# A plain first block pair in every feed-forward stage, with the Strassen sums of the activations made behind it

## The chip, the cores and the metric

The kernel runs on one core of a Trainium2 chip. Its engines work side by side and meet through semaphores: TensorE (PE in the profile) multiplies matrices, VectorE (DVE) and ScalarE (ACT) work element by element, GpSimd (POOL) does a little, and SyncE (SP) issues the DMAs from HBM to SBUF, the on-chip memory. Matmuls add up in PSUM. The metric is the device time of one execution in microseconds (us).

## What is computed

Two layers of an encoder, for one sequence of 512 tokens (`SEQ`) with 1024 channels (`D_MODEL`), all in float32. The change touches the feed-forward stages alone; there are four, two in each layer:

```python
FFN_HIDDEN = ((8 * D_MODEL // 3 + 255) // 256) * 256     # 2816

def swiglu(x, w_gate, w_up, w_down):
    return (jax.nn.silu(x @ w_gate) * (x @ w_up)) @ w_down

for l in range(DEPTH):                                   # DEPTH = 2
    h = x + 0.5 * swiglu(rms_norm(x, ffn1_norm[l]), ffn1_w_gate[l], ffn1_w_up[l], ffn1_w_down[l])
    z = rms_norm(h, mix_norm[l]) @ w_in[l]
    ...
    h = h + jnp.concatenate([y_sgu, y_mlstm], axis=-1) @ w_out[l]
    x = h + 0.5 * swiglu(rms_norm(h, ffn2_norm[l]), ffn2_w_gate[l], ffn2_w_up[l], ffn2_w_down[l])
return rms_norm(x, final_norm)
```

`rms_norm` multiplies by the gain g and by 1/sqrt(mean of squares + eps) of the token.

## The kernel before

**Numbers as two halves.** A float32 matrix is split in a rounded part (hi) and a remainder (lo), and a product is three matmuls: hi x hi, hi x lo, lo x hi. For weights the rounding is a cast on ACT (L144, to `whi` or `whix`) and the remainder a subtraction on DVE (L145, to `wlo` or `wlox`). The pairs `whix`/`wlox` and `whi`/`wlo` take turns, block by block; there are 2 buffers of the x kind and 3 of the other, 3 of `rawx` and 3 of `raw` for what the DMAs bring.

**Activations.** They lie transposed, channels on the partitions, in 8 tiles x[d] of 128 channels by 512 tokens. `Wide.split` (L351) takes them in twos, j = 0 to 3. With the gain multiplied in (`fa`, four pieces of 256 columns) it makes the blocks A11, A12, A22 as hi and lo (L367, L368), then four sums S1, S2, S4, S3 in `fb` (L369), and those as hi and lo (L374, L375).

**Pairs.** The hidden channels are worked in 11 pairs q of 256 channels. A pair computes gate and up products as a 2 x 2 block product in the form of Strassen and Winograd: seven block products of 24 matmuls with 256 columns each (`strassen`, L159 to L161), 168 matmuls, in three PSUM banks pa, pe, pb. The seven need sums of the four weight blocks (`combine`, L149; `pair_plan` yields e0 to e6 in the order in which they are used). A plain pair has eight block products, 192 matmuls, and needs none of the sums. The first stage's pair 0 is plain already (L1048 to L1062, finished by `gated_plain`). The others open with `strassen_pair(..., opening)`, which takes three block products together, first for j = 0, 1, 2, then for j = 3.

**Stage.** The pairs come in groups of 4, 4 and 3, each followed by eight down-projections `pd` (L206 to L208), which are added to x (L598). Four tiles on, the squares that the norm needs are summed on DVE (L293, `acc`); `rstd_tok` sums them over the channels on PE (`ss`, L304), takes the inverse root by Newton steps on 128 x 4 numbers (L222 to L224), puts it on a diagonal (`dg`, L312), and `spread` has PE broadcast it (`rb`, L317). In the first stage `rstd` (L328 to L336) does that on 128 x 512 numbers with a reciprocal.

**Order.** A tile framework puts the instructions of each engine in a row when the kernel is built, by its model of when each is ready; the engine then works its row strictly in order. `take()` hands out weight units and keeps a few more in preparation than are used (`AHEAD`).

Of the kernel before, what the change touches and what calls it, by code (L numbers as in the profile page):

```python
# [8 lines left out]
F32 = mybir.dt.float32  # L9
# [25 lines left out]
class Net:  # L35
    AHEAD = {"X": 4, "M": 2, "F": 2}
# [17 lines left out]
    def masks(self):  # L54
# [4 lines left out]
        make_identity(nc, self.ident)  # L59
        self.tri = []  # L60
# [280 lines left out]
A11, A12, A22, S3, S1, S2, S4 = range(7)  # L341


class Wide(Norm):
    def __init__(self, b, g):
        super().__init__(b, g)
        self.d = 0
        self.eng = b.nc.vector
        self.spread = None

    def split(self, x):  # L351
# [25 lines left out]
        self.last = fa  # L377
# [87 lines left out]
def strassen_pair(b, norm, rstd, opening):  # L465
# [29 lines left out]
    if spread is not None:  # L495
        spread()
# [6 lines left out]
    return halved(b, G, True), rstd  # L503


def pair_plan(blocks):
    st = {}

    def e0(b):
        st["b11"] = b.load(blocks[0])  # L510
        return b.halves(st["b11"])

    def e1(b):
        st["b12"] = b.load(blocks[1])
        b.combine(st["b11"], st["b12"], st["b11"])
        return b.halves(st["b11"])

    def e2(b):
# [653 lines left out]
```

## Time and profile before

| | us |
|---|---|
| median of 3 runs | 1793.61 (1792.57 to 1794.6) |
| the profiled execution | 1797.66 |
| its span | 1795.9 |
| PE busy | 1759.7 (98%) |
| DVE busy | 1396.1 (78%) |
| ACT busy | 868.7 (48%) |

Stage 1 begins its pairs at 7.26 us of the span, stage 2 at 544.05 (behind the output projection of the first mixer), stage 3 at 897.30 (behind the down-projections of stage 2), stage 4 at 1427.02. A group of rows below gives the window from there to the first down-projection for each; for stage 1 the window begins behind its plain pair, at 31.55. In windows, a name with (x) is busy time and number of instructions, PEclk the granted clock of TensorE as a share of full speed. In a timeline a row gives start, duration, engine, line, operation, what is written and read, and in brackets how long the engine had stood before and who released it.

### The profile page before, as it was taken

Reading aid. Unit: us, or ns where it says so; the run is one execution under the profiler, and the core shown is the slowest. Engines: PE = TensorE matmul, PEld = TensorE weight load, DVE = VectorE, ACT = ScalarE, POOL = GpSimd, SP = SyncE. Lnnn points to the kernel's source line nnn. Section 1 sums busy time; section 2 is a strip of 40 time slices with the busy share of each in tenths; the row PEclk is TensorE's granted clock in tenths of the full one; section 3 lists DMA queues with packets and bytes.
Section 4 is the critical chain, followed back from the end, with each engine's and each line's share of the span. In section 5 each row is a group of like instructions: output and inputs, shape, how many; then the busy total and the mean of one; then the engine's idle time right before and its main releaser. Section 6 shows DMA issues by size and latency. Waiting matters only on the chain.

```text
span 1795.9 us, 28343 instructions
## 1 busy us (share of the span) xinstructions
PE 1759.7 (98%) x11626; PEld 1610.3 (90%) x11626; DVE 1396.1 (78%) x2113; ACT 868.7 (48%) x1223; POOL 98.6 (5%) x164
## 2 busy tenths in 40 slices
PE   8999999999998999999989999999999999999998
PEld 8889989887888989989889899898888799899898
DVE  8967958667988957958889588595698989597685
ACT  7434424557555524525545244254576545254255
POOL 6100000103010000000010000002030000000000
PEclk9999999999998999999999999999999999999999
DMA  5332322321241333323323223223112224233223
GB/s 188 95 129 87 122 86 80 97 82 47 66 146 59 114 110 95 118 82 93 108 95 118 82 90 124 89 75 106 59 60 83 91 86 129 84 105 118 83 77 109
DMA packets 51394, 173.60 MB, mean 97 GB/s; under 512 B 5824, under 2 KB 7872, under 8 KB 51264
## 3 DMA queue, kind: packets, MB, share of 16 engines
q1 hardware_dynamic: 51264, 171.79, 29.9%
q8 instruction: 91, 1.49, 0.3%
q14 instruction: 39, 0.32, 0.1%
HBM read 169.67 MB, written 2.10 MB: 96 GB/s over the span
## 4 chain that ended last, share of the span: by engine, by line
PE 85%; DVE 9%; ACT 3%; issue 1%; DMA 1%; SPq 0%; POOL 0%; DVEq 0%; ACTq 0%; POOLq 0%
PE pd L206 9%; PE pd L208 9%; PE pd L207 9%; PE pb L159 6%; PE pb L160 6%; PE pb L161 6%; PE pe L160 4%; PE pa L159 4%; PE pa L160 4%; PE pe L159 4%; PE pa L161 4%; PE pe L161 4%; PE pm L206 3%; PE pm L207 3%; PE pm L208 3%
## 5 line engine op out<-in xcount | busy, mean ns | idle before, releaser
L179 ACT CAST whi<-raw 128x1024 fp32r<-128x1024 f32 (+2 forms) x157 | 151.9, 967 | 317.9 <-PE pd L207 157.5
L206 PE MATMUL pd<-hh,whi 128*128 128x512 f32 (+1 forms) x752 | 282.9, 377 | 0.4 <-ACT hh L448 0.4
L207 PE MATMUL pd<-hl,whi 128*128 128x512 f32 (+1 forms) x752 | 282.6, 376 | 0.6 <-DVE hl L449 0.6
L208 PE MATMUL pd<-hh,wlo 128*128 128x512 f32 (+1 forms) x752 | 282.6, 376 | 0.5 <-DVE wlo L180 0.5
L180 DVE TENSOR_TENSOR wlo<-raw,whi 128x1024 fp32r<-128x1024 f32 (+2 forms) x157 | 176.4, 1125 | 30.0 <-ACT whi L179 29.1
L598 DVE SCALAR_TENSOR_TENSOR x<-pd,x 128x512 f32<-128x512 f32 x88 | 60.7, 690 | 152.1 <-PE pd L208 152.0
L206 PEld LDWEIGHTS pd<-hh,whi 128*128 128x128 f32 x752 | 141.4, 188 | 29.5 <-ACT hh L448 4.3
L208 PEld LDWEIGHTS pd<-hh,wlo 128*128 128x128 f32 x752 | 141.6, 188 | 26.0 <-DVE wlo L180 0.8
L207 PEld LDWEIGHTS pd<-hl,whi 128*128 128x128 f32 x752 | 141.6, 188 | 26.0 <-DVE hl L449 0.8
L144 ACT CAST whi<-rawx 128x1024 fp32r<-128x1024 f32 x86 | 88.6, 1048 | 150.1 <-DVE rawx L149 92.0
L159 PE MATMUL pb<-xh,whix 128*128 128x256 f32 x528 | 153.2, 290 | 4.3 <-ACT u L482 3.4
L161 PE MATMUL pb<-xh,wlox 128*128 128x256 f32 x528 | 151.3, 287 | 0.6 <-DVE wlox L145 0.6
L160 PE MATMUL pb<-xl,whix 128*128 128x256 f32 x528 | 151.3, 286 | 0.0
L144 ACT CAST whix<-rawx 128x1024 fp32r<-128x1024 f32 x86 | 89.8, 1049 | 114.8 <-PE pb L160 80.1
L159 PE MATMUL pb<-xh,whi 128*128 128x256 f32 x504 | 142.2, 282 | 0.1
L160 PE MATMUL pb<-xl,whi 128*128 128x256 f32 x504 | 142.1, 282 | 0.0
L161 PE MATMUL pb<-xh,wlo 128*128 128x256 f32 x504 | 141.5, 281 | 0.5 <-DVE wlo L145 0.5
L144 ACT CAST whi<-raw 128x1024 fp32r<-128x1024 f32 x64 | 67.1, 1048 | 103.0 <-issue 40.5
L145 DVE TENSOR_TENSOR wlo<-rawx,whi 128x1024 fp32r<-128x1024 f32 x86 | 105.1, 1222 | 9.2 <-ACT whi L144 8.9
L145 DVE TENSOR_TENSOR wlox<-rawx,whix 128x1024 fp32r<-128x1024 f32 x86 | 105.0, 1221 | 9.1 <-ACT whix L144 9.1
L159 PEld LDWEIGHTS pb<-xh,whix 128*128 128x128 f32 x528 | 103.0, 195 | 5.8 <-ACT u L482 4.2
L159 PE MATMUL pe<-xh,whi 128*128 128x256 f32 x352 | 101.9, 290 | 5.4 <-ACT xh L374 5.4
(331 smaller groups left out, 5065.7 us busy)
## 6 DMA issues: line engine op xcount, KB each, us to landing
rawx<-in_wst SPq DMA_DIRECT2D x86, 512.0 KB, 3.6
raw<-in_wst SPq DMA_DIRECT2D x86, 512.0 KB, 3.6
raw<-in_wd SPq DMA_DIRECT2D x64, 512.0 KB, 3.6
raw<-in_wd SPq DMA_DIRECT2D x37, 384.0 KB, 3.1
raw<-in_win SPq DMA_DIRECT2D x24, 512.0 KB, 3.5
raw<-in_wo SPq DMA_DIRECT2D x16, 512.0 KB, 3.5
raw<-in_wv SPq DMA_DIRECT2D x8, 512.0 KB, 3.5
x<-in_xT SPq DMA_DIRECT2D x8, 256.0 KB, 4.0
```

What stands on the lines that cost most here:

```text
L144: self.copied = nc.scalar.copy(hi, raw)
L145: nc.vector.tensor_tensor(out=lo, in0=raw, in1=hi.bitcast(F32), op=ALU.subtract)
L159: nc.tensor.matmul(o, whi[:, j, i, :], hi, start=f, stop=False, skip_group_check=True)
L160: nc.tensor.matmul(o, whi[:, j, i, :], lo, start=False, stop=False, skip_group_check=True)
L161: nc.tensor.matmul(o, wlo[:, j, i, :], hi, start=False, stop=j == 3, skip_group_check=True)
L179: self.copied = nc.scalar.copy(hi[:, r], raw[:, r])
L180: nc.vector.tensor_tensor(out=lo[:, r], in0=raw[:, r], in1=hi[:, r].bitcast(F32), op=ALU.subtract)
L206: nc.tensor.matmul(ps, whi[:, k0 + k, :], xh, start=k == 0, stop=False)
L207: nc.tensor.matmul(ps, whi[:, k0 + k, :], xl, start=False, stop=False)
L208: nc.tensor.matmul(ps, wlo[:, k0 + k, :], xh, start=False, stop=k == n - 1)
L598: nc.vector.scalar_tensor_tensor(out=xd, in0=pd, scalar=0.5, in1=xd, op0=ALU.mult, op1=ALU.add)
```

## The change

- Pair 0 of every feed-forward stage is plain (`plain_plan`, `plain_step`, `plain_banks`). The blocks come in the x kind, the other, the x kind, the other. The low half of the fourth activation block, `a21`, is made in `split` from the `hy` pool.
- `split` makes no sums. `sums()` is called after the plain pair and makes them in place in `fa`: two subtractions and two scalar_tensor_tensor of 256 columns for each j, then the cast and the remainder as before.
- `rstd_tok` is called behind `sums` in all stages; `between`, with `spread` and `gated_plain`, runs in pair 1 behind its first block product.
- Signs: the weights' sums are additions, and U is made with scalar_tensor_tensor, two per pair. The count of weight steps is the same.
- `AHEAD` for "X" is 5, and `eye()` makes the identity earlier. `rawx` is taken by b11 and b22, `raw` by b12 and b21. `add` is defined and not called.

```diff
-    AHEAD = {"X": 4, "M": 2, "F": 2}
+    AHEAD = {"X": 5, "M": 2, "F": 2}
...
-    def load(self, src):
-        raw = self.rawx()
+    def load(self, src, chain=False):
+        raw = (self.phase.tile([P, 1024], F32, tag="rawx", name="rawx", bufs=3) if chain else
+               self.wp.tile([P, 1024], F32, tag="raw", name="raw"))
...
-    def combine(self, out, a, c):
-        self.nc.vector.tensor_tensor(out=out, in0=a, in1=c, op=ALU.subtract)
...
-A11, A12, A22, S3, S1, S2, S4 = range(7)
+A11, A12, A22, S3, S2, S4, S1 = range(7)
...
-        fb = b.wide("fb").rearrange("p (q t) -> p q t", q=4)
+        if d % 4 == 1:
+            self.a21 = b.pair(F32R, "a21").rearrange("p k (l t) -> p k l t", l=2)
+        a21 = self.a21[:, d // 2 % 2]
         nc.scalar.copy(hi[:, 0:3], fa[:, 1:4])
+        nc.scalar.copy(a21[:, 0], fa[:, 0])
         nc.vector.tensor_tensor(out=lo[:, 0:3], in0=fa[:, 1:4], in1=hi[:, 0:3].bitcast(F32), op=ALU.subtract)
-        sub = lambda o, a, c, op=ALU.subtract: nc.vector.tensor_tensor(out=fb[:, o - S3], in0=a, in1=c, op=op)
-        sub(S1, fa[:, 0], fa[:, 3], ALU.add)
-        sub(S2, fb[:, S1 - S3], fa[:, 1])
-        sub(S4, fa[:, 2], fb[:, S2 - S3])
-        sub(S3, fa[:, 1], fa[:, 0])
-        nc.scalar.copy(hi[:, 3:7], fb)
-        nc.vector.tensor_tensor(out=lo[:, 3:7], in0=fb, in1=hi[:, 3:7].bitcast(F32), op=ALU.subtract)
+        nc.vector.tensor_tensor(out=a21[:, 1], in0=fa[:, 0], in1=a21[:, 0].bitcast(F32), op=ALU.subtract)
         self.xs.append((hi, lo))
+        self.low.append((a21[:, 0], a21[:, 1]))
+
+    def sums(self):
+        nc = self.b.nc
+        for fa, (hi, lo) in zip(self.fas, self.xs):
+            f = lambda i: fa[:, i - S3]
+            nc.vector.tensor_tensor(out=f(S1), in0=f(S1), in1=f(S3), op=ALU.subtract)
+            nc.vector.tensor_tensor(out=f(S3), in0=f(S2), in1=f(S3), op=ALU.subtract)
+            for o, a, m in ((S2, f(S1), f(S2)), (S4, f(S4), f(S2))):
+                nc.vector.scalar_tensor_tensor(out=f(o), in0=a, scalar=-1.0, in1=m, op0=ALU.mult, op1=ALU.subtract)
+            nc.scalar.copy(hi[:, 3:7], fa)
+            nc.vector.tensor_tensor(out=lo[:, 3:7], in0=fa, in1=hi[:, 3:7].bitcast(F32), op=ALU.subtract)
...
+def plain_banks(b):
+    return [b.bank("mm", "pm") for _ in range(2)], [b.bank("sm", "pm") for _ in range(2)]
+
+def plain_step(b, norm, j, blocks, banks):
+    nc = b.nc
+    pg, pu = banks
+    hi, lo = norm.xs[j]
+    for k, out, second in ((0, pg, False), (1, pu, False), (3, pg, True), (2, pu, True)):
+        whi, wlo = blocks[k]
+        for i in range(2):
+            for th in range(2):
+                o = out[i][:, th * 256:(th + 1) * 256]
...
+                nc.tensor.matmul(o, whi[:, j, i, :], xh, start=f, stop=False, skip_group_check=True)
+                nc.tensor.matmul(o, whi[:, j, i, :], xl, start=False, stop=False, skip_group_check=True)
+                nc.tensor.matmul(o, wlo[:, j, i, :], xh, start=False, stop=second and j == 3, skip_group_check=True)
...
-def strassen_pair(b, norm, rstd, opening):
+def strassen_pair(b, norm, get, between=None):
...
-    three = ((pa, A11), (pe, S1), (pb, S2))
-    if opening:
-        ws = [b.take() for _ in three]
-        for js in (range(3), (3,)):
-            for (p, idx), w in zip(three, ws):
-                b.strassen(p, w, X, idx, True, js)
-    else:
-        for p, idx in three:
-            b.strassen(p, b.take(), X, idx, True)
+    b.strassen(pa, b.take(), X, A11, True)
+    if between is not None:
+        between()
+    b.strassen(pe, b.take(), X, S1, True)
+    b.strassen(pb, b.take(), X, S2, True)
...
-    nc.vector.tensor_tensor(out=U[:, 1], in0=q(pb), in1=q(e5), op=ALU.add)
-    nc.vector.tensor_tensor(out=U[:, 0], in0=q(pe), in1=q(u2), op=ALU.add)
+    nc.vector.scalar_tensor_tensor(out=U[:, 1], in0=q(pb), scalar=-1.0, in1=q(e5), op0=ALU.mult, op1=ALU.subtract)
+    nc.vector.scalar_tensor_tensor(out=U[:, 0], in0=q(pe), scalar=-1.0, in1=q(u2), op0=ALU.mult, op1=ALU.subtract)
...
+    def step(fetch, low, sums=()):
+        def make(b):
+            if fetch:
+                st[fetch] = b.load(srcs[fetch], fetch in ("b11", "b22"))
+            for t in sums:
+                add(b, *t)
+            return b.halves(st[low])
+        return make
+
+    return [step("b11", "b11"), step("b12", "b11", [("b11", "b11", "b12")]),
+            step("b22", "b11", [("b11", "b11", "b22")]), step(None, "b22"),
+            step(None, "b12", [("b12", "b12", "b22")]), step("b21", "b21"),
+            step(None, "b11", [("b11", "b11", "b21")])]
+
+def plain_plan(blocks):
+    def whole(k):
+        return lambda b: b.halves(b.load(blocks[k], k % 2 == 0))
+    return [whole(k) for k in range(4)]
...
-            if q == 0 and first is not None:
-                rstd = norm.rstd()
-                hs += gated_plain(b, *first, rstd)
+            if q == 0:
+                banks = first
+                if banks is None:
+                    blocks = [b.take() for _ in range(4)]
+                    banks = plain_banks(b)
+                    for j in range(4):
+                        plain_step(b, norm, j, blocks, banks)
+                norm.sums()
+                rstd["full"], _, spread = norm.rstd_tok()
+
+                def between():
+                    spread()
+                    hs.extend(gated_plain(b, *banks, rstd["full"]))
+
                 continue
-            h, rstd = strassen_pair(b, norm, rstd, q == 0)
-            hs += h
+            hs.extend(strassen_pair(b, norm, lambda: rstd["full"], between if q == 1 else None))
```

Where instructions stand in stage 2 (stages 3 and 4 are alike), first DVE. Before, from the last j of `split` on; `fb` are the sums, `xl` the remainders of blocks (768 columns) and sums (1024), L145 the remainders of weights:

```order
L369 TENSOR_TENSOR fb<-fa 128x256 x2
L368 TENSOR_TENSOR xl<-fa,xh 128x768
L369 TENSOR_TENSOR fb<-fb,fa 128x256
L293 TENSOR_TENSOR acc<-acc,sq 128x512
L369 TENSOR_TENSOR fb<-fa,fb 128x256
L145 TENSOR_TENSOR wlo<-raw,whi 128x1024
L145 TENSOR_TENSOR wlox<-raw,whix 128x1024
L375 TENSOR_TENSOR xl<-fb,xh 128x1024
L149 TENSOR_TENSOR raw<-raw,rawx 128x1024
L481 TENSOR_TENSOR pb<-pb,s_5644 128x512
L145 TENSOR_TENSOR wlo<-rawx,whi 128x1024
L145 TENSOR_TENSOR wlox<-raw,whix 128x1024
```

In the change (its lines are numbered anew: L384 is the remainder of the sums, L379 to L382 the sums, L146 the remainder of a weight block, L534 an addition of weight blocks), from the last two j's sums on:

```order
L379 TENSOR_TENSOR fa<-fa 128x256 x2
L380 TENSOR_TENSOR fa<-fa 128x256 x2
L382 SCALAR_TENSOR_TENSOR fa<-fa 128x256 x4
L384 TENSOR_TENSOR xl<-fa,xh 128x1024 x2
L146 TENSOR_TENSOR wlox<-rawx,whix 128x1024
L534 TENSOR_TENSOR rawx<-rawx,raw 128x1024
L534 TENSOR_TENSOR raw<-raw,rawx 128x1024
L146 TENSOR_TENSOR wlo<-rawx,whi 128x1024 x2
L534 TENSOR_TENSOR rawx<-rawx 128x1024
L307 TENSOR_SCALAR nv_5798<-ss 128x4
L146 TENSOR_TENSOR wlo<-raw,whi 128x1024
```

The sums now stand together behind the remainders of the plain pair's blocks and activations, and ahead of everything for pair 1, whose first remainder is `wlox<-rawx,whix`.

Further on DVE, the end of the statistics before, with `dg` the diagonal for `rb`:

```order
L224 SCALAR_TENSOR_TENSOR rtok<-nt_5688,rtok 128x4
L492 TENSOR_TENSOR U<-pb,e_5645 128x512
L312 TENSOR_SCALAR dg<-ident,rtok 128x128 x4
L145 TENSOR_TENSOR wlox<-rawx,whix 128x1024
L149 TENSOR_TENSOR rawx<-rawx 128x1024
```

and in the change:

```order
L222 SCALAR_TENSOR_TENSOR nt_5800<-nt_5800,nv_5798 128x4
L223 SCALAR_TENSOR_TENSOR rtok<-nt_5800,rtok 128x4
L146 TENSOR_TENSOR wlox<-rawx,whix 128x1024
L311 TENSOR_SCALAR dg<-ident,rtok 128x128 x4
L508 TENSOR_TENSOR pb<-pb,s_5925 128x512
L464 TENSOR_TENSOR G<-pm,rstd 128x512 x2
```

Before, `dg` stood behind a U of pair 0; now it stands behind the remainder of the last weight block (e6) of pair 1.

On PE, around the broadcast `rb`, before (pb is a block product of pair 0):

```order
L160 MATMUL pa<-xl,whi 128x256
L161 MATMUL pa<-xh,wlo 128x256
L159 MATMUL pb<-xh,whix 128x256
L160 MATMUL pb<-xl,whix 128x256
L161 MATMUL pb<-xh,wlox 128x256
L159 MATMUL pb<-xh,whix 128x256
L160 MATMUL pb<-xl,whix 128x256
L161 MATMUL pb<-xh,wlox 128x256
L317 MATMUL rb<-dg,ones 128x512
L159 MATMUL pb<-xh,whix 128x256
```

and in the change, in pair 1, where the pb rows are the end of the third block product (S2) and the pe rows the second (S1):

```order
L158 MATMUL pb<-xl,whix 128x256
L159 MATMUL pb<-xh,wlox 128x256
L157 MATMUL pa<-xh,whi 128x256
L158 MATMUL pa<-xl,whi 128x256
L159 MATMUL pa<-xh,wlo 128x256
L316 MATMUL rb<-dg,ones 128x512
L157 MATMUL pe<-xh,whi 128x256
L158 MATMUL pe<-xl,whi 128x256
L159 MATMUL pe<-xh,wlo 128x256
```

`rb` has gone from the middle of pair 0's block products to behind pa and pb of pair 1, ahead of its pe.

## Rows read from the trace of the kernel before

**Rows 1.** The page's busy line, whole span: us, share, number of instructions.

```profile
PE 1759.7 (98%) x11626; PEld 1610.3 (90%) x11626; DVE 1396.1 (78%) x2113; ACT 868.7 (48%) x1223; POOL 98.6 (5%) x164
```

**Rows 2.** Windows: openings of stages 2, 3, 4 and 1, and steady pairs.

```profile
core 0: us, PE busy (x) PEld busy (x) DVE busy (x) ACT busy (x) POOL busy (x), PEclk, DMA share, GB/s
544.05:637.16 93.11, 87.65 (x683) 85.29 (x682) 85.11 (x105) 48.23 (x58) 0.00 (x0) 0.95 0.32 102
897.30:988.19 90.89, 86.24 (x683) 84.08 (x682) 81.90 (x102) 45.44 (x54) 6.93 (x19) 0.96 0.33 105
1427.02:1520.49 93.47, 87.99 (x684) 85.69 (x682) 84.91 (x105) 48.16 (x58) 0.00 (x0) 0.95 0.33 102
31.55:104.93 73.38, 66.28 (x510) 63.91 (x508) 69.04 (x69) 35.76 (x40) 19.50 (x33) 0.95 0.33 102
690.00:750.00 60.00, 60.00 (x508) 60.00 (x507) 55.80 (x56) 30.54 (x35) 0.00 (x0) 1.00 0.31 97
```

**Rows 3.** Windows: stretches at granted clock 0.50, stages 2, 2, 3 and 1.

```profile
549.70:556.53 6.83, 5.24 (x24) 4.66 (x23) 6.83 (x12) 3.94 (x7) 0.00 (x0) 0.50 0.21 80
559.94:563.35 3.41, 3.41 (x16) 3.41 (x17) 2.50 (x3) 0.41 (x1) 0.00 (x0) 0.50 0.52 154
908.10:914.93 6.83, 5.74 (x24) 5.30 (x25) 3.59 (x4) 2.69 (x4) 6.66 (x19) 0.50 0.25 80
54.77:61.59 6.82, 6.08 (x28) 6.08 (x29) 5.41 (x6) 1.41 (x3) 0.00 (x0) 0.50 0.35 113
```

**Rows 4.** Waits of PE, 544 to 566 us: total us, times, longest.

```profile
PE pe L159 <- ACT xh L374: 2.6, 2, 2.0
PE pe L160 <- DVE xl L375: 0.9, 1, 0.9
PE pa L160 <- DVE xl L368: 0.9, 1, 0.9
PE pa L159 <- ACT xh L367: 0.9, 1, 0.9
```

**Rows 5.** Groups of DVE by line and shape: count, busy us and mean ns, idle before.

```profile
L145 DVE TENSOR_TENSOR wlox<-rawx,whix 128x1024 fp32r<-128x1024 f32 x86 | 105.0, 1221 | 9.1 <-ACT whix L144 9.1
...
L293 DVE TENSOR_TENSOR acc<-acc,sq 128x512 f32<-128x512 f32 x28 | 19.6, 699 | 0.0
...
L369 DVE TENSOR_TENSOR fb<-fa 128x256 f32<-128x256 f32 x32 | 13.1, 428 | 4.6 <-ACT fa L360 4.2 <-ACT fa L363 0.3
...
L278 DVE SCALAR_TENSOR_TENSOR xlo<-x,g,xhi 128x512 fp32r<-128x512 f32 x16 | 11.9, 746 | 0.0
```

**Rows 6.** Timeline of ACT and DVE: a weight block waiting for its buffer, stage 2.

```profile
557.87 1.04 ACT L144 CAST whix<-raw 128x1024 fp32r<-128x1024 f32 x1 [4.23 <-PE pa L160]
...
558.95 1.23 DVE L145 TENSOR_TENSOR wlox<-raw,whix 128x1024 fp32r<-128x1024 f32 x1 [1.82 <-ACT whix L144]
```

**Rows 7.** Timelines of PE and DVE, stage 2: the statistics, and full-width steps behind them.

```profile
569.03 0.95 PE L304 MATMUL ss<-ones,acc 128*128 128x1 f32 x8
569.84 0.36 PE L159 MATMUL pb<-xh,whix 128*128 128x256 f32 x1
...
570.88 0.16 DVE L222 TENSOR_TENSOR nt<-rtok 128x4 f32<-128x4 f32 x1
571.08 0.16 DVE L223 SCALAR_TENSOR_TENSOR nt<-nt,nv 128x4 f32<-128x4 f32 x1
...
573.60 0.87 DVE L312 TENSOR_SCALAR dg<-ident,rtok 128x128 f32<-128x128 f32 x4
...
575.63 1.23 DVE L149 TENSOR_TENSOR rawx<-rawx 128x1024 f32<-128x1024 f32 x1
576.77 1.22 DVE L497 TENSOR_TENSOR U<-U,rstd 128x1024 f32<-128x1024 f32 x1
...
574.61 1.10 PE L317 MATMUL rb<-dg,ones 128*128 128x512 f32 x2
575.14 0.68 PE L159 MATMUL pb<-xh,whix 128*128 128x256 f32 x1
```

**Rows 8.** Timeline of DVE, stage 1: the reciprocal.

```profile
38.94 3.34 DVE L336 RECIPROCAL rstd<-nt 128x512 f32<-128x512 f32 x1
```

More of the change, by code (lines that the diff above doesn't have):

```diff
@@ L52, in __init__, with eye @@
         nc.vector.memset(self.ones, 1.0)
-    def masks(self):
+    def eye(self):
         nc, c = self.nc, self.const
@@ L59, in masks @@
         make_identity(nc, self.ident)
+    def masks(self):
+        nc, c = self.nc, self.const
         self.tri = []
@@ L348, in __init__ @@
         self.eng = b.nc.vector
-        self.spread = None
+        self.fas, self.low = [], []
     def split(self, x):
@@ L462, in gated_plain @@
     return halved(b, g)
-def strassen_pair(b, norm, rstd, opening):
+def plain_banks(b):
[9 more added lines that the diff above has]
+                o = out[i][:, th * 256:(th + 1) * 256]
+                if not second and th:
+                    xh, xl = norm.low[j]
+                else:
+                    idx = (A22 if th else A12) if second else A11
+                    xh, xl = hi[:, idx, :], lo[:, idx, :]
+                f = j == 0 and not second and th == 0
+                nc.tensor.matmul(o, whi[:, j, i, :], xh, start=f, stop=False, skip_group_check=True)
+                nc.tensor.matmul(o, whi[:, j, i, :], xl, start=False, stop=False, skip_group_check=True)
+                nc.tensor.matmul(o, wlo[:, j, i, :], xh, start=False, stop=second and j == 3, skip_group_check=True)
+def strassen_pair(b, norm, get, between=None):
     nc = b.nc
@@ L483, in strassen_pair @@
     b.strassen(pe, b.take(), X, S4, False)
-    spread = None
-    if rstd is None:
-        rstd, _, spread = norm.rstd_tok()
     b.strassen(pb, b.take(), X, S3, False)
+    rstd = get()
     U = b.wide("U").rearrange("p (t i c) -> p t i c", t=2, i=2)
@@ L502, in strassen_pair, with add @@
     nc.vector.tensor_tensor(out=G, in0=G, in1=U, op=ALU.mult)
-    return halved(b, G, True), rstd
+    return halved(b, G, True)
 def pair_plan(blocks):
+    srcs = dict(zip(("b11", "b12", "b22", "b21"), blocks))
     st = {}
[L509 to L518, printed above, removed]
-        st["b22"] = b.load(blocks[2])
-        b.combine(st["b11"], st["b22"], st["b11"])
-        return b.halves(st["b11"])
-    def e3(b):
-        return b.halves(st["b22"])
-    def e4(b):
-        b.combine(st["b12"], st["b22"], st["b12"])
-        return b.halves(st["b12"])
-    def e5(b):
-        st["b21"] = b.load(blocks[3])
-        return b.halves(st["b21"])
-    def e6(b):
-        b.combine(st["b21"], st["b21"], st["b11"])
-        return b.halves(st["b21"])
-    return [e0, e1, e2, e3, e4, e5, e6]
+    def add(b, out, a, c):
+        b.nc.vector.tensor_tensor(out=st[out], in0=st[a], in1=st[c], op=ALU.add)
+    def step(fetch, low, sums=()):
[14 more added lines that the diff above has]
+    return [whole(k) for k in range(4)]
 def one(src, width=P):
@@ L547, in ffn_plan @@
         for q in range(m0 // 2, (m0 + nk) // 2):
-            if q > 0 or not first:
-                yield from pair_plan([wst[q, k] for k in range(4)])
+            blocks = [wst[q, k] for k in range(4)]
+            if q > 0:
+                yield from pair_plan(blocks)
+            elif not first:
+                yield from plain_plan(blocks)
         for d in range(ND):
@@ L571, in ffn @@
     nc = b.nc
-    rstd = None
+    rstd = {}
     hooks = hooks or {}
@@ L1036, in trunk_kernel @@
     raws = [b.load_parts() for _ in range(4)]
-    pg, pu = [b.bank("mm", "pm") for _ in range(2)], [b.bank("sm", "pm") for _ in range(2)]
+    blocks = [tuple(t.rearrange("p (j i c) -> p j i c", j=4, i=2) for t in r[1:]) for r in raws]
+    banks = plain_banks(b)
     for j in range(4):
@@ L1041, in trunk_kernel @@
             cur.split(x[:, d, :])
-        a21 = b.slot(F32R, name="a21").rearrange("p (k t) -> p k t", k=2)
-        nc.scalar.copy(a21[:, 0, :], cur.last[:, 0, :])
-        nc.vector.tensor_tensor(out=a21[:, 1, :], in0=cur.last[:, 0, :], in1=a21[:, 0, :].bitcast(F32), op=ALU.subtract)
-        hi, lo = cur.xs[j]
         for k in range(4):
             b.fill((wst[0, 0, k].rearrange("p j i c -> p (j i c)"), *raws[k]), j * 256, (j + 1) * 256)
-        for k, banks in ((0, pg), (1, pu), (3, pg), (2, pu)):
-            s = k in (2, 3)
-            whi, wlo = (t.rearrange("p (j i c) -> p j i c", j=4, i=2) for t in raws[k][1:])
-            for i in range(2):
-                for th in range(2):
-                    o = banks[i][:, th * 256:(th + 1) * 256]
-                    if not s and th:
-                        xh, xl = a21[:, 0, :], a21[:, 1, :]
-                    else:
-                        idx = (A22 if th else A12) if s else A11
-                        xh, xl = hi[:, idx, :], lo[:, idx, :]
-                    f = j == 0 and not s and th == 0
-                    nc.tensor.matmul(o, whi[:, j, i, :], xh, start=f, stop=False, skip_group_check=True)
-                    nc.tensor.matmul(o, whi[:, j, i, :], xl, start=False, stop=False, skip_group_check=True)
-                    nc.tensor.matmul(o, wlo[:, j, i, :], xh, start=False, stop=s and j == 3, skip_group_check=True)
+        plain_step(b, cur, j, blocks, banks)
+    b.eye()
     held = {}
```

23 lines of the change are left out of this document (9 added, 14 removed).

## The prediction

> **What bounds the kernel now.** I first read the busy line: TensorE (PE) is busy in 98% of the span [rows 1]. So a change can gain only in the stretches where PE waits or runs slowly, and each matmul it adds is paid in full. Next comes what a matmul costs: in a steady stretch of pairs 508 matmuls take 60.00 us [rows 2], 118.1 ns each; I use 118.75, as some records there belong to 512-column matmuls. 24 (one block product) are 2.85 us, a Strassen pair of 168 is 19.95, a plain pair of 192 is 22.8.
>
> Then the four openings, from a stage's first pair to its first down-projection [rows 2]. Without waits one in stages 2 to 4 would take 672 x 0.11875 = 79.80, plus the statistics sums `ss` (0.81 between neighbours) and the spread `rb` (0.53), 81.14 us together [rows 7]. The windows are 93.11, 90.89 and 93.47, so **11.97, 9.75 and 12.33 us are lost, 34.05 in all**. In stage 1 the lost part is 73.38 - 504 x 0.11875 - 0.56 = 12.97.
>
> [...] PE waits 2.6 + 0.9 + 0.9 + 0.9 = 5.3 us for `xh` and `xl`, the products of `Wide.split` [rows 4]. [...]
>
> **The extra product.** Pair 0 of stages 2 to 4 becomes plain: 24 matmuls more, on PE, with nothing to hide them. 3 x 2.85 = **8.55 us lost**. [...]
>
> **The sums leave the opening.** The plain pair needs A11, A12, A22 and the low half of the fourth block, all made by the casts and remainders before the sums. By the order these are ready in DVE's queue well before PE wants them: the last j comes at about 548 us on the clock of before, and PE, starting at 544.05, reaches it after 144 matmuls at 561. So the plain pair runs through and ends at 544.05 + 22.8 = 566.85. All the 5.3 us of waits [rows 4] and their half-clock stretches [rows 3] go: of the 11.97 only the gaps behind the first pair stay, 0.5. **Gained: 34.05 - 1.5 = 32.55.** The sums themselves (per j four of about 0.43, a cast of 1.04, a remainder of 1.22 [rows 5, 6]) are done by about 556, under the plain pair.
>
> **What is late next: the weights.** The next weight block, e0 of pair 1, needs a `whix` buffer; there are two, and both hold blocks of the plain pair, because that pair uses all four blocks for each j and frees the first only in its last quarter, after matmul 156, at 544.05 + 18.5 = 562.6. DVE and ACT have been standing since about 556, DVE at the remainder `wlox` of e0, with everything for pair 1 queued behind it in order. The kernel before already shows this link: ACT's cast of `whix` idled 4.23 us until PE released the buffer, and DVE's remainder 1.82 us for that cast [rows 6]. Now I walk the queues. A cast takes 1.05 (564.87 for the first remainder's end with its 1.22), and each full-width DVE step 1.14 from start to start [rows 7]: remainder e0, two additions, remainders e1 and e3, an addition, remainder e5, remainder e2. The last, the eighth, is there at about 564.87 + 7 x 1.14 + 0.2 = 573.05. PE after the plain pair: `ss` to 567.7, block product e0 (pa) to 570.5, and then, as the order puts it, e2 (pb), ahead of e1, which has been ready for longer. It waits for cast and remainder 1.28 + 1.03 us: **2.3 us idle**; e2 ends at 575.7. Behind that stands `rb`, which needs `dg`. On DVE that comes after remainder e4, an addition, nine small steps of 0.2 [rows 7], remainder e6, and dg itself (0.87): 573.05 + 1.14 x 2 + 1.8 + 1.14 + 0.87 = 579.2. PE has three matmuls in between and waits from 576.0 to 579.25: **3.25 us**. With gaps of 0.4 that makes **5.95 us per opening, 17.85 in three**. The pairs behind then have margins of 0.3 to 0.5 us per block and I count no more waits. Bounds: nothing, if buffers come free earlier than I read; 10 us, if the margins break as well.
>
> **The clock behind these waits.** The trace of before does not show this stall pattern. Its nearest rows are stalls of 2 to 3.4 us, after which 3.41 or 6.83 us ran at half [rows 3]. Two stalls of 2.3 and 3.25 us stand 3.2 us apart. Bounds: no such stretch, or one of each length as in stage 2 (5.1 lost). I take one of 3.41 per opening, 1.7 lost, **5.1 in three**, since these stalls are the size of the shorter ones of before.
>
> **Stage 1.** It already has a plain pair. It exchanges the reciprocal of 3.34 us [rows 8] and its steps on 512 columns for the short statistics on 4 columns, but puts the eight weight steps behind `nv`. Walked in the same way: PE waits some 6.2 us for the remainder of e2 from 35 to 41, 1.4 after that and 0.6 for `rb`, has one half-clock stretch (3.4 lost) and small gaps of 0.7: 12.3 instead of 12.97. **Gain 0.7**, bounds -2.5 and +3.
>
> **Edits that I cost at nothing.** Additions for subtractions in the weights have the same count and shape. U as scalar_tensor_tensor: the row with two fp32 sources from SBUF is 746 ns at 512 columns against 699 for tensor_tensor [rows 5], so at most 0.05 per step on DVE, which is busy 55.80 of 60 us in the steady stretch [rows 2]; with two steps per pair it fits. If DVE's slack went, 0.1 per pair x 40 would be 4 us. Taking five weight blocks ahead instead of four moves loads forward in SP's queue; the DMA engines are busy 0.31 of the steady stretch [rows 2], so no transfer is squeezed by it.
>
> [...] Each opening makes eight of its sums as scalar_tensor_tensor on two fp32 sources, and if such an operation took twice as long as the plain sum of 428 ns [rows 5], the eight would add 8 x 0.43 = 3.4 us to DVE. In stages 2 to 4 DVE would still be done before 562.6; in stage 1 the sums stand before the weights, and PE would be up to 3.4 us later. [...] This trace speaks against it: 746 against 699 ns [rows 5].
>
> **The sum.** 32.55 - 8.55 - 17.85 - 5.1 + 0.7 = **1.75 us faster**. It is made on the profiled execution (1797.66 us, span 1795.9), which lies 4 us above the median of 1793.61; none of its terms depends on that, so I take it from the median: **1791.9 us**. This kernel's measurement can tell about 0.2% (3.6 us) from no change, so the forecast is "the same".
>
> **Rivals.**
> - A, the clock stays up. No half-clock stretch behind the two short waits: 5.1 us more gain, 1786.8. For it: e2's work stands between the two stalls; against it: short stalls of 2 us were followed by slow stretches in every opening of before.
> - B, the weights are in time. The release of `whix` does not hold pair 1 and PE runs on: 32.55 - 8.55 + 0.7 = 24.7, 1768.9. Against it: two buffers in the code, and the 4.23 us [rows 6].
> - C, slower: the stalls keep the clock down as in stage 2 of before, 6.83 + 3.41 us at half in each opening, 5.1 lost instead of 1.7. The sum falls by 10.2, to 1802.1. It decides from a loss to the clock of 2.3 us per opening (4.6 us at half rate), where the sign turns; beyond 3.5 it is slower by over 0.2%. For it: stage 2 and two stalls as here; against it: stage 3 had one stretch only.
> - D, scalar_tensor_tensor at half speed: stage 1 loses up to 3.4, 1795.3.
> - E, the change does not do what it says: scheduled so that the sums still stand in front of the plain pair. Then the 5.3 us per opening stay and 8.55 comes on top: 1802. The order shows the sums behind the first blocks' remainders, so I give it next to nothing.
>
> **How the numbers follow.** Forecast 0.40, A 0.26, B 0.07, C with E 0.22, D 0.05. Faster by over 0.2% (under 1790.0): A, B and a little of the forecast's lower side, 0.36. Slower (over 1797.2): C and a little of the upper side, 0.23. Within: 0.41. The range goes from A's less stage 1's upper bound, 1784, to C's, 1801, and leaves out B and the worst of C. The likeliest case's own range is 1788 to 1797.
>
> **What would show it.** Right: in the windows of stages 2 to 4 (first matmul of the plain pair to first down-projection) 90 to 93 us with 24 matmuls more; no wait of PE for `xh` or `xl` made by the sums; ACT idle before `whix` of pair 1 for some 6 us, released by a matmul of the plain pair; a PE wait of 1 to 2.5 us at pb for `wlox` or `whix`, and one of 3 at `rb` for `dg`. Stage 1: a wait of some 6 us behind the first product of pair 1. Wrong: pair 1 starting with no wait (B), granted clock 0.50 for over 5 us in an opening (C) or never (A), waits in pairs 2 to 4 (the margins), or sums that take 0.8 us each (D).

## The result, and the profile after

| | before | changed |
|---|---|---|
| median (us) | 1793.14 (4 runs) | 1805.81 (1803.68 to 1807.45, 4 runs) |
| profiled execution / its span | 1797.66 / 1795.9 | 1803.68 / 1802.0 |
| PE busy | 1759.7 | 1767.0 |
| mean granted clock of the profile | 0.989 | 0.993 |

The changed kernel is **slower: ratio 1.0069, 95% interval 1.0051 to 1.0086**, some 12.7 us. The forecast was 1791.9 with a range up to 1801: the time lies above it. The two profiled executions stand only 6.0 us apart; why the medians stand 12.7 apart and the profiles 6.0 has to be explained too.

The openings of the changed kernel, as in [rows 2], from the first matmul of the plain pair (in stage 1 from its end) to the first down-projection, in the order stage 2, 3, 4, 1, and then the four half-clock stretches inside the first three and the one of stage 1, as in [rows 3] (columns as there):

```profile
544.92:637.37 92.45, 87.81 (x708) 85.59 (x707) 77.35 (x100) 44.22 (x52) 0.00 (x0) 0.98 0.25 82
898.77:992.59 93.82, 89.27 (x708) 87.10 (x707) 73.55 (x94) 40.31 (x47) 6.82 (x19) 0.96 0.27 84
1432.69:1525.12 92.43, 87.78 (x709) 85.56 (x707) 78.11 (x101) 44.42 (x52) 0.00 (x0) 0.98 0.27 84
31.73:104.77 73.04, 65.72 (x517) 63.86 (x516) 68.07 (x83) 35.56 (x40) 23.49 (x37) 0.93 0.33 102
...
580.46:583.87 3.41, 3.41 (x11) 2.38 (x11) 1.32 (x3) 1.63 (x2) 0.00 (x0) 0.50 0.44 144
928.62:932.03 3.41, 3.41 (x18) 3.41 (x17) 3.10 (x12) 0.00 (x0) 0.00 (x0) 0.50 0.56 144
935.44:938.86 3.42, 3.30 (x9) 2.27 (x10) 1.24 (x3) 0.58 (x1) 0.00 (x0) 0.50 0.57 153
1467.92:1471.34 3.42, 3.26 (x9) 2.26 (x10) 1.18 (x3) 1.16 (x2) 0.00 (x0) 0.50 0.58 155
37.74:47.98 10.24, 4.97 (x21) 4.67 (x22) 10.24 (x20) 3.16 (x4) 10.24 (x12) 0.50 0.35 98
```

The first three windows hold 24 matmuls more than those of [rows 2]. In stages 2 and 4 they are shorter all the same, 92.45 us against 93.11 and 92.43 against 93.47; in stage 3 the window is 2.93 us longer, 93.82 against 90.89. PE's waits in stage 2's opening are other ones than in [rows 4]. Columns: total us, times, longest:

```profile
PE pa L157 <- ACT s L506: 1.5, 1, 1.5
PE pb L157 <- ACT whix L145: 1.3, 1, 1.3
PE rb L316 <- DVE dg L311: 1.0, 1, 1.0
PE pb L159 <- DVE wlox L146: 0.8, 1, 0.8
```

No wait for `xh` or `xl` is left. Instead PE waits for `whix` and `wlox` of pair 1, for the copy of pa to s1, and at `rb`. DVE and ACT, timelines of the same opening, show where that comes from:

```profile
564.61 1.23 DVE L146 TENSOR_TENSOR wlox<-rawx,whix 128x1024 fp32r<-128x1024 f32 x1 [7.12 <-ACT whix L145]
...
572.93 1.23 DVE L146 TENSOR_TENSOR wlox<-rawx,whix 128x1024 fp32r<-128x1024 f32 x1
...
579.28 0.87 DVE L311 TENSOR_SCALAR dg<-ident,rtok 128x128 f32<-128x128 f32 x4
...
563.53 1.05 ACT L145 CAST whix<-rawx 128x1024 fp32r<-128x1024 f32 x1 [7.49 <-PE pm L492]
...
577.06 1.04 ACT L145 CAST whix<-rawx 128x1024 fp32r<-128x1024 f32 x1 [3.21 <-PE pb L158]
578.01 0.58 ACT L506 COPY s<-pa 128x512 f32<-128x512 f32 x1
```

ACT idled 7.49 us until a matmul of the plain pair (`pm`) gave the x buffer back, DVE 7.12 for that cast, and then the chain of weights runs to `dg` at 579.28. The copy of pa to s1 stands on ACT behind a later cast, which waited 3.21 us for pb.

What the openings do not show is in the groups behind them. Windows from the first matmul of the second group of stage 2 to that of the third, and from there to the end of the stage, pairs and down-projections with no half-clock stretch in them, of the kernel before and then of the changed one:

```profile
680.97:804.58 123.61, 123.61 (x866) 115.78 (x864) 93.01 (x92) 50.98 (x56) 0.00 (x0) 1.00 0.33 103
804.58:897.30 92.72, 92.72 (x650) 86.83 (x648) 79.06 (x92) 50.72 (x64) 0.00 (x0) 1.00 0.31 97
```

```profile
680.87:805.39 124.52, 124.43 (x865) 116.04 (x864) 92.39 (x93) 51.16 (x56) 0.00 (x0) 1.00 0.34 102
805.39:898.77 93.38, 93.31 (x650) 86.99 (x648) 79.86 (x94) 52.08 (x70) 0.00 (x0) 1.00 0.38 116
```

The same matmuls at full clock take 0.91 and 0.66 us longer. The other stages do the same, about 1.6 us a stage, **6.4 us in all: more than the whole difference of the two profiles (6.0)**. These groups have no plain pair and make no sums of the activations. Of what the change says, only the signs, the use of `raw` and `rawx` and the fifth block ahead reach them.

There PE's block products, unbroken before, are cut. In the second pair of stage 2's second group the order is pa, pe, pb, pe, 12 matmuls of pa, pb, the other 12 of pa, pb; in the next pair 5 of pa, pe, pb, 19 of pa. The first pair of a group is uncut. In each of the others PE stands once, at the first cut: three times in this group and twice in the third. Over the whole changed kernel PE's weight loads wait for the copies of pb (u2) and pe (e5) as follows, 17 and 9 times, in the kernel before 5 and 3 times; columns: total us, times, longest:

```profile
PEld pb L157 <- ACT u L509: 4.2, 17, 0.3
PEld pe L157 <- ACT e L507: 1.9, 9, 0.2
```

The hole at 713.5 in detail, in timelines of the changed kernel, PE's weight loads and matmuls and then DVE and ACT:

```profile
713.40 0.19 PEld L159 LDWEIGHTS pa<-xh,wlo 128*128 128x128 f32 x1
713.86 0.19 PEld L157 LDWEIGHTS pb<-xh,whix 128*128 128x128 f32 x1 [0.27 <-ACT u L509]
...
713.52 0.28 PE L159 MATMUL pa<-xh,wlo 128*128 128x256 f32 x1
713.86 0.39 PE L157 MATMUL pb<-xh,whix 128*128 128x256 f32 x1
714.09 0.28 PE L158 MATMUL pb<-xl,whix 128*128 128x256 f32 x1
...
709.03 1.22 DVE L146 TENSOR_TENSOR wlo<-rawx,whi 128x1024 fp32r<-128x1024 f32 x1
710.17 1.22 DVE L456 TENSOR_TENSOR hl<-G,hh 128x1024 fp32r<-128x1024 f32 x1
711.31 1.22 DVE L146 TENSOR_TENSOR wlox<-rawx,whix 128x1024 fp32r<-128x1024 f32 x1
712.44 0.69 DVE L508 TENSOR_TENSOR pb<-pb,s 128x512 f32<-128x512 f32 x1
...
713.22 0.59 ACT L509 COPY u<-pb 128x512 f32<-128x512 f32 x1 [2.67 <-DVE pb L508]
```

The third product (pb) ended at 709.38. Before S3 may be added into pb, DVE must add s1 to it and ACT copy it to u2. On DVE three full-width steps stand ahead of the addition, which starts at 712.44, 3.06 us after it could. PE fills with half of A12, then waits; from 713.52 to 713.86 is 0.34 us in place of 0.12, and the matmul behind the hole takes 0.23 to the next. In the kernel before, in the same pair, the third product ended at 709.47, and one step was in front:

```profile
709.11 1.23 DVE L149 TENSOR_TENSOR raw<-raw,rawx 128x1024 f32<-128x1024 f32 x1
710.26 0.69 DVE L481 TENSOR_TENSOR pb<-pb,s 128x512 f32<-128x512 f32 x1
```

So the first question is which part of the change put two more steps there.

### The profile page after: what moved, and what is told of

The parts are those of the page before. It is cut to its first block, busy times and chain, and to the rows that moved or that the text cites. A ratio compares the mean times of both kernels' runs of the same rounds, so it can differ in the third digit from the quotient of the medians.

```text
span 1802.0 us, 28586 instructions
## 1 busy us (share of the span) xinstructions
PE 1767.0 (98%) x11706; PEld 1614.5 (90%) x11706; DVE 1365.1 (76%) x2108; ACT 855.5 (47%) x1215; POOL 92.1 (5%) x164
## 4 chain that ended last, share of the span: by engine, by line
PE 88%; DVE 6%; ACT 3%; issue 1%; DMA 1%; POOL 0%; SPq 0%; DVEq 0%; ACTq 0%; POOLq 0%
PE pd L205 9%; PE pd L207 9%; PE pd L206 9%; PE pb L157 6%; PE pb L159 6%; PE pb L158 6%; PE pe L157 4%; PE pm L205 4%; PE pm L207 4%; PE pm L206 4%; PE pe L158 4%; PE pe L159 4%; PE pa L158 4%; PE pa L159 4%; PE pa L157 4%
## 5 line engine op out<-in xcount | busy, mean ns | idle before, releaser
L145 ACT CAST whix<-rawx 128x1024 fp32r<-128x1024 f32 x106 | 110.5, 1050 | 186.1 <-PE pb L158 100.8
L145 ACT CAST whi<-rawx 128x1024 fp32r<-128x1024 f32 x100 | 102.8, 1047 | 133.0 <-DVE rawx L534 76.3
L146 DVE TENSOR_TENSOR wlox<-rawx,whix 128x1024 fp32r<-128x1024 f32 x106 | 128.7, 1221 | 31.8 <-ACT whix L145 31.7
L157 PE MATMUL pb<-xh,whix 128*128 128x256 f32 x480 | 139.9, 291 | 11.0 <-ACT whix L145 10.3
L159 PE MATMUL pb<-xh,wlox 128*128 128x256 f32 x480 | 137.7, 287 | 3.1 <-DVE wlox L146 3.1
L158 PE MATMUL pb<-xl,whix 128*128 128x256 f32 x480 | 137.3, 286 | 0.0
L146 DVE TENSOR_TENSOR wlo<-rawx,whi 128x1024 fp32r<-128x1024 f32 x100 | 121.0, 1223 | 16.6 <-ACT whi L145 16.6
L157 PEld LDWEIGHTS pb<-xh,whix 128*128 128x128 f32 x480 | 93.1, 194 | 15.5 <-ACT whix L145 11.1
L534 DVE TENSOR_TENSOR rawx<-rawx,raw 128x1024 f32<-128x1024 f32 x80 | 97.7, 1222 | 1.2
L159 PEld LDWEIGHTS pb<-xh,wlox 128*128 128x128 f32 x480 | 93.2, 194 | 4.0 <-DVE wlox L146 4.0
```

The costliest lines, as they stand in the source:

```text
L145: self.copied = nc.scalar.copy(hi, raw)
L146: nc.vector.tensor_tensor(out=lo, in0=raw, in1=hi.bitcast(F32), op=ALU.subtract)
L157: nc.tensor.matmul(o, whi[:, j, i, :], hi, start=f, stop=False, skip_group_check=True)
L158: nc.tensor.matmul(o, whi[:, j, i, :], lo, start=False, stop=False, skip_group_check=True)
L159: nc.tensor.matmul(o, wlo[:, j, i, :], hi, start=False, stop=j == 3, skip_group_check=True)
L534: b.nc.vector.tensor_tensor(out=st[out], in0=st[a], in1=st[c], op=ALU.add)
```

## The experiments

**The fifth block ahead, undone and alone.**

```diff
-    AHEAD = {"X": 5, "M": 2, "F": 2}
+    AHEAD = {"X": 4, "M": 2, "F": 2}
```

> The changed kernel with one edit undone: weight blocks are taken four ahead again instead of five. Theory Q (queue order): the fifth block ahead puts one more weight step before the copies of pa, pe and pb on ACT and before pb + s1 on DVE; in the steady pairs of the changed kernel PE then stands 0.2 to 0.3 us for such a copy once or twice a pair and its block products stand in cut pieces. In the profile the two steady groups of a stage lost 0.98 and 0.43 us, 5.6 us in four stages. With four ahead the cuts of these groups are gone, so groups of 79.8 and 59.9 us as in the kernel before, and 1805.8 - 5.6 = about 1800 us. Rival S (signs): the scalar_tensor_tensor steps and the other use of rawx and raw make the copies late; then the groups stay at 80.8 and 60.3 and the time at 1805.8.

Measured: 1789.49 us (10 runs), ratio to before 0.9983 (0.9974 to 0.9993): **16.3 us below the changed kernel, and below the kernel before**. The window of the same two groups:

```profile
675.90:799.46 123.56, 123.56 (x866) 115.77 (x864) 92.64 (x93) 51.17 (x56) 0.00 (x0) 1.00 0.34 103
```

The holes are gone, as theory Q has it. But 16.3 is far over the 5.6 expected. The openings gained too: 89.03, 89.84 and 90.87 us in stages 2, 3 and 4 in place of 92.45, 93.82 and 92.43, with one half-clock stretch (3.41 us, stage 4) in these three where the changed kernel had four.

The same edit put into the kernel before (4 to 5):

> The kernel before with only the fifth weight block ahead. Theory Q: the holes of 0.2 to 0.3 us in the steady pairs appear here too, some 5 to 6 us in eight groups, so about 1799 us, 0.3% slower than before. Rival S: no holes, 1793.

Measured: 1798.96 us, ratio 1.0027 (1.0016 to 1.0038), 6.0 us over before. Its steady group at stage 3 shows the hole again:

```profile
1032.88:1157.32 124.44, 124.28 (x865) 116.05 (x864) 92.49 (x92) 51.07 (x56) 0.00 (x0) 1.00 0.33 103
```

The steady groups of its profile are 5.5 us longer than those of before in all. So the fifth block does it by itself, with the old signs and the old openings. S falls for these holes.

**Where the 16 us lie.** Five ahead in the first group of each stage only, and in the other two only:

```diff
+        b.AHEAD = dict(b.AHEAD, X=5 if gi == 0 else 4)
...
+        b.AHEAD = dict(b.AHEAD, X=4 if gi == 0 else 5)
```

> The changed kernel with five blocks ahead only in the first group of each stage (the opening with the plain pair) and four in the other two. The changed kernel lost 16.3 us against the run with four ahead everywhere. By the profiles 6.5 of it lie in the steady groups, the rest in the openings: waits of rb for dg, cut products, and half-clock stretches behind them. Theory Q: this run keeps the openings' part, 1789.5 + 10 = about 1799, with uncut groups of 79.8 and 59.9 us.

> The counterpart: four ahead in the first group of each stage and five in the other two. Theory Q: the holes of 0.2 to 0.3 us in the steady groups alone, 1789.5 + 6.5 = about 1796, with groups of some 80.8 and 60.5 us, and openings as with four ahead. Rival: the two parts do not add, one of these runs holds nearly all of the 16 us.

Measured: 1800.08 us (10.6 over four ahead) and 1797.93 us (8.4 over). Together that is 19.0, against 16.3 with five ahead everywhere. Stage 2 of the first (second group, then opening) and the second group of the other:

```profile
680.82:804.38 123.56, 123.56 (x866) 115.78 (x864) 93.09 (x93) 51.17 (x56) 0.00 (x0) 1.00 0.32 102
544.96:637.32 92.36, 87.72 (x709) 85.49 (x707) 77.19 (x100) 44.15 (x52) 0.00 (x0) 0.98 0.28 83
```

```profile
679.81:804.30 124.49, 124.39 (x865) 116.01 (x864) 91.95 (x93) 51.18 (x56) 0.00 (x0) 1.00 0.34 104
```

In the steady groups the loss stands where five are ahead and not where four are. The openings are less clean. Stage 2's opening with four ahead, first in the run with five in the other groups and then in the run with four everywhere:

```profile
545.59:636.08 90.49, 86.89 (x707) 85.78 (x706) 77.39 (x100) 43.89 (x52) 0.00 (x0) 0.98 0.27 84
543.15:632.18 89.03, 85.41 (x707) 84.32 (x706) 77.20 (x100) 43.80 (x52) 0.00 (x0) 1.00 0.28 86
```

PE's and ACT's instructions have the same order in both; the first has a stretch of 3.41 us at 0.50, the second has none. In its profile that run is 9.5 us above the run with four ahead, 6.5 of it in the steady groups and 2.9 in the openings of all four stages, though four are ahead in these. As far as one execution of each shows, that is the 2.7 by which the two parts come to more than the whole.

With five ahead in the openings `rb` waits for `dg` (gone with four), products are cut in every pair of the group, and longer stretches run at 0.50. In the profiles the three openings take 279.87 us in place of 269.74, and 13.66 us more of them run at 0.50. Counted at half, as the prediction counts a stretch (1.7 us of 3.41), up to 6.8 of the 10.1 us are the clock's and the rest is stall: an estimate, which no run separates.

**The signs alone**, in the kernel before:

```diff
-        sub(S1, fa[:, 0], fa[:, 3], ALU.add)
+        nc.vector.tensor_tensor(out=F(S1), in0=fa[:, 3], in1=fa[:, 0], op=ALU.subtract)
+        nc.vector.scalar_tensor_tensor(out=F(S2), in0=F(S1), scalar=-1.0, in1=fa[:, 1], op0=ALU.mult, op1=ALU.subtract)
...
-    nc.vector.tensor_tensor(out=U[:, 1], in0=q(pb), in1=q(e5), op=ALU.add)
+    nc.vector.scalar_tensor_tensor(out=U[:, 1], in0=q(pb), scalar=-1.0, in1=q(e5), op0=ALU.mult, op1=ALU.subtract)
```

> The kernel before with the signs alone: additions for the weights' sums, b11 and b22 in rawx and b12 and b21 in raw, two of the four sums of each j and both U of a pair by scalar_tensor_tensor. The openings stay Strassen, four blocks ahead. If the signs cost nothing, as the prediction had it, 1793, and the steady groups 79.8 and 59.9 us; if scalar_tensor_tensor were half as fast, the opening's 8 sums would take 0.8 us each and the time would be 1800 or more.

Measured: 1792.27 us, ratio 0.9992 (0.9983 to 1.0000). The signs cost nothing. The groups of the changed kernel (count, busy us and mean ns, idle before) say the same of each step:

```profile
L382 DVE SCALAR_TENSOR_TENSOR fa<-fa 128x256 f32<-128x256 f32 x32 | 13.0, 423 | 0.3
L379 DVE TENSOR_TENSOR fa<-fa 128x256 f32<-128x256 f32 x16 | 6.6, 423 | 0.0
```

423 ns either way: the 0.8 us that the expectation weighs for each sum is not seen in these rows. On 512 columns the operation took 688 ns for U (L518 of the changed kernel, one source in PSUM) and 746 for `xlo` (both in SBUF) [rows 5].

**The x buffers.** Four ahead, and the plain pair's blocks in one x buffer (the second block) and three of the other kind:

```diff
-    def halves(self, raw):
+    def halves(self, raw, x=None):
...
-        if self.wturn % 2:
+        if (self.wturn % 2) if x is None else x:
...
-        return lambda b: b.halves(b.load(blocks[k], k % 2 == 0))
+        return lambda b: b.halves(b.load(blocks[k], k % 2 == 0), k == 1)
```

> The run with four ahead, and the four blocks of the plain pairs of stages 2 to 4 put into one x buffer (second block) and three of the other kind, so that the first block of pair 1 finds a free x buffer. Theory W (weights held up by whix): the wait of PE for whix and wlox of pair 1 (1.3 + 0.8 us per opening in the changed kernel) goes, and part of the half-clock stretch behind it; rb, which stands ahead of the second block product and behind the last weight block on DVE, still holds PE for 2 to 3 us. So 2 to 4 us per opening, 6 to 12 in three, against the run with four ahead: 1788 to 1794. Rival: the buffer was not what ended last (the sums of the activations or the DMAs were), then no change against the run with four ahead.

Measured: 1783.42 us, 6.1 below four ahead, the low end of what was expected. The waits of stage 2's opening, with four ahead and then with the buffers as well:

```profile
PE pa L157 <- ACT s L506: 1.5, 1, 1.5
PE pb L157 <- ACT whix L145: 1.3, 1, 1.3
PE pb L159 <- DVE wlox L146: 0.8, 1, 0.8
```

```profile
PE pa L157 <- ACT s L506: 1.5, 1, 1.5
PE rb L316 <- DVE dg L311: 1.0, 1, 1.0
```

The waits at pb are gone, so they were the buffer's. PE arrives earlier at `rb` and now waits there.

**`rb` later, without the buffers.**

```diff
     b.strassen(pa, b.take(), X, A11, True)
-    if between is not None:
-        between()
     b.strassen(pe, b.take(), X, S1, True)
     b.strassen(pb, b.take(), X, S2, True)
+    if between is not None:
+        between()
```

> The run with four ahead, and the call that issues rb and finishes the plain pair moved behind the third block product of pair 1; on PE the second product then stands ahead of the third and both ahead of rb. Theory: PE's waits in the opening (whix and wlox 2.5 us, copy s 1.8) come from the order in which pair 1 is taken up; with the second product between, 2.85 us of work stand where PE waited, so 2 to 3 us per opening and the half-clock stretch with it: 1780 to 1784. Rival: the queue of DVE simply ends later and the wait moves to the third product or to rb: 1789 as with four ahead.

Measured: 1796.35 us, **6.9 above** four ahead: a miss, worse even than the rival. On PE the product pe did fill the wait for the weights, but the waits gathered in one place. Waits of PE in stage 2's opening, and the end of the statistics on DVE there:

```profile
PE rb L316 <- DVE dg L311: 3.9, 1, 3.9
PE pa L157 <- ACT s L506: 1.5, 1, 1.5
...
578.15 1.22 DVE L534 TENSOR_TENSOR raw<-raw,rawx 128x1024 f32<-128x1024 f32 x1
579.29 0.16 DVE L223 SCALAR_TENSOR_TENSOR rtok<-nt,rtok 128x4 f32<-128x4 f32 x1
...
580.07 0.88 DVE L311 TENSOR_SCALAR dg<-ident,rtok 128x128 f32<-128x128 f32 x4
```

`dg` ends 38.1 us after the opening begins, where it ends after 34.0 with four ahead alone: DVE's chain still begins with the late buffer, and steps of the next weights now stand between the small ones. PE has less left to do meanwhile: 3.9 us in one piece, and a half-clock stretch of 6.83 us behind it in each of the three openings.

**Both, and in stage 1 too**, then with other numbers ahead:

```diff
-    def load_parts(self):
+    def load_parts(self, x):
...
-        if self.wturn % 2:
+        if x:
...
-    raws = [b.load_parts() for _ in range(4)]
+    raws = [b.load_parts(k == 1) for k in range(4)]
```

> Four ahead, the plain blocks in one x buffer and three others (in stage 1 too), and rb moved behind the third block product. If the two edits remove different waits, this is below both: each opening of stages 2 to 4 loses under 3 us instead of 5 to 7, 1775 to 1780. Stage 1 waited 6.4 us for whix behind its first product; if the buffer held that cast, another 3 to 6 us. Rival: in stage 1 the cast waits for DVE's chain of weight sums behind the activations' sums, and the buffers change nothing there.

Measured: 1775.64 us, ratio 0.9896 (0.9884 to 0.9909). The opening of stage 2 and its clock:

```profile
543.36:628.31 84.95, 84.85 (x708) 84.12 (x706) 77.26 (x102) 44.48 (x52) 0.00 (x0) 1.00 0.30 95
```

81.14 + 2.85 = 83.99 is this window's work; 0.96 us is lost of what was 8.2 in the changed kernel (92.45 - 83.99, less one down-projection matmul of 0.23 that stands before the boundary there). No stretch at half clock is left in the openings of stages 2 to 4. Stage 1 is not helped: its window from the first matmul is 97.11 us, 97.01 with four ahead alone and 96.47 with `rb` later. The rival was right there. In the changed kernel the x buffer held the first cast of stage 1 for 0.45 us only, against 7.49 in stage 2:

```profile
27.53 1.05 ACT L145 CAST whix<-rawx 128x1024 fp32r<-128x1024 f32 x1 [0.45 <-PE pm L492]
```

DVE works there without a pause from the sums of the activations, whose last remainder ends at 34.1 us, through the weights to `dg` at 46.9, and PE waits for that row of work.

> The run with the buffers and rb moved, at five ahead. If the openings' part of the loss came from the weights chain that the buffers mend, only the steady holes stay: 1775.6 + 6.5 = 1782. If five ahead spoils the opening by itself: 1790 or more.

> The same with three blocks ahead. By the order theory fewer blocks ahead leave the copies earlier in the queues: the cut block products of the openings become fewer (in the order the group behind the opening has two cuts less), so 0 to 3 us below four ahead; the steady groups are uncut with both, no difference there. Rival: with three ahead the weights come late and PE waits for casts or remainders in the steady groups: slower by some us.

> The run with the buffers and rb moved, at two ahead. In the order the openings are cut once less than with three. If lateness of the copies is all that counts, 1771 to 1773; if the weights of the steady groups come too late, waits of PE for casts or remainders and 1780 or more.

Measured: five ahead 1781.41 us, four 1775.64, three 1773.50, **two 1772.82 us, ratio 0.9887 (0.9873 to 0.9900)**, the fastest kernel here and 20 us under the one before. With the chain mended, five ahead costs 5.8 us, about the holes of the steady groups alone; what it cost in the openings hung on the waits that the buffers and the later `rb` take away together. Three and two are not told apart. In the pairs of stages 2 to 4 PE waits for no cast and no remainder, even at two; in stage 1's opening it does, for 3.8 us (2.9 at four).

**The kernel before once more**, for the clock:

> The kernel before once more, unchanged, for a second profile and the granted clock of several executions. Its profiled execution took 1797.66 us where the median is 1793.1. Theory C: the executions differ by how much of the openings runs at half clock; so time and mean granted clock go together, some 1.8 us for each 0.001 of clock over a span of 1796 us at half the rate, and the median run has a mean clock of about 0.991 or 0.992 against the 0.989 of the profile. Rival: the clock is the same in all and the difference is profiling.

Measured: 1793.71 us (11 runs). Three executions had a mean clock of 0.989 and spans of 1794.3 to 1795.9 us, the other eight 0.991 to 0.993 and 1789.2 to 1792.8. The profile on which the prediction rests, 1795.9 at 0.989, belongs to the longest of these, at the lowest mean clock. If the lower mean comes from stretches at 0.50, and half of each is lost, a mean lower by 0.004 is an estimated 7.2 us of 1796; 6.7 lie between the two ends (1789.2 at 0.993, 1795.9 at 0.989). Of the changed kernel's four executions the profiled one is the fastest (span 1802.0 at 0.993; the others 1803.3 to 1805.7 at 0.989 to 0.992).

## Why the prediction failed, step by step

**The extra product: right.** The plain pair of stage 2 takes 22.81 us (192 matmuls), 22.8 forecast, without a wait. That is 118.8 ns each. The reason given for 118.75 was wrong: the window 690 to 750 holds no 512-column matmul, its count takes in matmuls that overlap its edges. From 680.97 to 760.78 us, 672 matmuls take 118.8 ns each.

**The sums leave the opening: right.** No wait for `xh` or `xl`; DVE idles 7.12 us after them.

**The weights: right in cause and size.** The x buffer was given back as the walk said, the cast 1.3 us late at pb (1.28), the remainder 0.8 (1.03). At `rb` 1.5 + 1.0 us were lost where one wait of 3.25 was forecast: part of it was the copy of pa to s1, behind a cast that waits for pb on ACT, which the walk had left out. In all 4.6 us of waits stand against 5.55.

**The clock behind: nearly right.** One stretch of 3.41 us each in stages 2 and 4 as taken, two in stage 3. Rival C decides from 2.3 us lost per opening; by the prediction's halving stage 3 came to 3.4, the others to 1.7. That half of a stretch is lost, 1.7 us of 3.41, from which the 5.1 of the sum comes, no run shows: in [rows 3] 16 matmuls run in 3.41 us, 0.21 us each in place of 0.12, so such a stretch costs about 1.5, by estimate. In the sum of profiles the three openings with their down-projections came out 0.3 us longer than before (409.19 us in three, from the plain pair's first matmul to the second group's, against 408.87), where 1.1 shorter was forecast.

**Stage 1: right by cancelling.** It waited 6.4 us for `whix` (6.2), but ran 10.24 us at half clock where one stretch of 6.8 was taken. Its second group begins at 148.27 us of the span in place of 148.97, 0.7 earlier, as forecast; in the window that the forecast used only 0.34 is gained (73.04 against 73.38). The agreement is luck. Its waits have another end than those of the other stages, as the run with both edits shows.

**Edits costed at nothing: here it failed.** The signs did cost nothing. Five blocks ahead were costed by SP and the DMAs alone, and their cost was not there: `take()` also issues the cast and the remainder of the block that it fetches, and those stood ahead of what PE's next product needed on DVE and ACT. That is 6.4 us in the steady groups by the profiles (8.4 by the medians of the run with five ahead there, whose openings ran longer as well), and 16.3 us with the openings. The prediction asked what the edit moves in SP's queue and not what it moves in those of DVE and ACT. The holes come from the place of steps in a row, with DVE no busier: 92.39 us of work in the group against 93.01. The margins of 0.3 to 0.5 us that it named for the pairs behind were considered in the openings only. Without this edit the rest of the change is 3.1 us faster than before (0.9983), where 1.75 was forecast. That nearness is partly luck: in the profiles the three openings with their down-projections gain 8.2 us with four ahead (400.68 against 408.87), where 1.05 was forecast, and the 4.5 us by which before's profile lies over its median take about half of that back.

**The base: a second fault.** The text said that none of the terms depends on the profiled execution lying 4 us above the median. The half-clock stretches do: they are part of the 34.05 us, and executions near the median ran at a mean clock of 0.991 to 0.992; that they have fewer such stretches is an estimate from that, as none of them was profiled. The account closes with it: from -1.75 to +6.0 between the profiles 6.4 (steady groups) + 1.4 (openings); then 4.5 because before's profile lies over its median, and 2.1 because the changed kernel's lies under its own, gives 12.7.

**The rivals.** None named what happened; C's price was near (1802), its mechanism holds in stage 3 alone, so that nearness is luck.

## What to carry to other kernels

A number that says how far ahead operands are prepared is not a matter of DMAs alone: every unit prepared ahead puts its vector work in the queues in front of the short steps that hand a result on (the fifth block cost 16.3 us here), so compare the order of the engines in the steady part as well, where one hole of 0.3 us repeats. A move that gives PE other work during a wait was worth nothing here while the chain that it waits for began as late as before; free the chain first, then move. And a sum with clock losses in it has to be set against several executions, not the one that was profiled.

## What the hardware showed beyond what was expected

Executions of one kernel differ by several us, and the granted clock with them: spans of 1789.2 us at 0.993 and 1795.9 at 0.989 in the kernel before. Where the stalls were gone from the openings of stages 2 to 4, no stretch at 0.50 remained in these and the mean clock rose to 0.996 to 0.997; the four executions of that kernel spread over 1.9 us (1774.16 to 1776.03), the eleven of the kernel before over 6.7 (1791.01 to 1797.71). In the steady groups the hole of 0.22 us shown above costs PE 0.33, since the matmul behind it takes 0.23 us to the next instead of 0.12.
